# Second MLP product by seven block products in place of eight, with the residual kept in DRAM

## Chip, core and metric

The kernel runs on one core of one Trainium2 chip. The metric is device microseconds of one execution; the value is the median of three runs. All times below are microseconds (us) unless marked ns. PE is the matrix engine (TensorE), PEld its weight loads, DVE is VectorE, ACT is ScalarE, POOL is GpSimd, and SP (SyncE) issues nearly all DMA transfers.

## What is computed

One decoder layer in float32: 512 tokens, 1024 channels. Three token mixers and an output projection come first; the change lies behind them, in the residual and the MLP of 4096 hidden columns.

```python
    x = x + rms_norm(merged @ w_out[l], g_mix_post[l])
    h = rms_norm(x, g_ff_pre[l])
    ff = jnp.square(jax.nn.relu(h @ w_ff_in[l])) @ w_ff_out[l]
    x = x + rms_norm(ff, g_ff_post[l])
```

## The kernel before

**Products.** Each operand is split into two float32r parts, hi (a cast on ACT) and lo (the rest, by a subtraction on DVE). `mm3` makes a product of three matmuls: hi·hi, hi·lo, lo·hi, each with 128 rows of contraction, 128 output rows and 512 output columns.

**Weights.** `plan` lists all weights in the order of use, in chunks of 512 KB. `load_chunk` loads a chunk into one of three buffers `raw` (RAW = 3); `split_chunk` makes `whi` (ACT) and `wlo` (DVE) in one of six buffer pairs (HL = 6) and then asks for the next load, which takes the `raw` buffer just read. `Weights` splits three chunks ahead of the one in use (AHEAD = 3).

**MLP.** The hidden columns are taken in four blocks b of 1024. The first product of a block (PSUM tile `psf`, eight tiles f of 128 hidden columns by 512 tokens, 24 matmuls each) goes through `ff_act`: relu on ACT, square on DVE, split into `ah` and `al`. The second product (PSUM tile `acc`) runs over two column halves and four token tiles of 128, 192 matmuls a block; `ff_done` adds each result into `ys` in SBUF. After the last block, each token tile is scaled by its root mean square and added to `x1`, the residual, which stays in SBUF from the output projection to the end. In block 0 the first four tiles f run by token halves, since the second 256 tokens are still being normed.

**Order.** PE takes its instructions in program order throughout; ACT and DVE do so from the second half of the output projection until tile f = 3 of block 0 (`act.on = dve.on = False` ends it). From there a scheduler sets their order, which is then fixed: each engine runs its queue in that order. Buffers are rings: slots `main`, `out` and `tmp` (12 slots for temporaries) in SBUF, eight banks in PSUM. Everything that goes through the recording helper has line 77.

Of the kernel before, what the change touches and what calls it, by code (L numbers as in the profile page):

```python
# [48 lines left out]
def trunk_layer(ctx: ExitStack, tc: tile.TileContext, x, w_in, w_pool, pool_scale, gm_gain,  # L49
# [8 lines left out]
    sb = ctx.enter_context(tc.tile_pool(name="sb", bufs=1))  # L58
    sm = ctx.enter_context(tc.tile_pool(name="sm", bufs=4))

    # One slot is [128, 512] of four bytes; a tag is a ring of slots that later phases take over.
    RINGS = {"main": 18, "out": 16, "tmp": 12, "nb": 2, "be": 2}

    def slot(ring, name, dt=F32):
        return sb.tile([P, T], dt, name=name, tag=ring, bufs=RINGS[ring])

    class InOrder:
        """An engine that, while `on`, takes its instructions in the order of this program."""
# [31 lines left out]

    def plan_cols(w, c0, n=256):
# [43 lines left out]
    for b in range(NB):  # L145
        for f in range(0, FT, 2):
            use["f1", b, f] = plan_cols(ff_in_k, (b * FT + f) * P)
        for hf in range(2):
            use["f2", b, hf] = plan_cols(ff_out_k[:, b * FT:(b + 1) * FT, :], hf * 512, 512)
# [12 lines left out]
    def split_chunk(engines="v"):  # L162
        raw = loaded[len(made)]
        hi = wp.tile([P, CHUNK], F32R, name="whi", bufs=HL)
        lo = wp.tile([P, CHUNK], F32R, name="wlo", bufs=HL)
        for n, e in enumerate(engines):
            c = slice(n * CHUNK // len(engines), (n + 1) * CHUNK // len(engines))
            act.copy(hi[:, c], raw[:, c])
            (nc.gpsimd if e == "p" else dve).tensor_sub(lo[:, c], raw[:, c], hi[:, c].bitcast(F32))  # L169
        at = 0  # L170
        outs = []
        for v in plan[len(made)]:
            _, a, b = v.shape
            outs.append(tuple(t[:, at:at + a * b].rearrange("p (a b) -> p a b", a=a)
                              for t in (hi, lo)))
            at += a * b
        made.append(outs)
        if len(loaded) < len(plan):
            load_chunk()

    class Weights:
        """The k tiles of one use; its chunks, and AHEAD more, are split as they come up."""
# [9 lines left out]
        def __getitem__(self, k):  # L192
            i, j = self.tiles[k]
            live = self.chunks.start if self.keep else i
            while len(made) < min(len(plan), i + 1 + self.ahead, live + HL):
                split_chunk()
            h, l = made[i][self.part]
            return h[:, j, :], l[:, j, :]

# [1 line left out]
    def split(src, hi, lo, scale=None):  # L201
        """hi, lo <- src (times a per-partition scale) in two float32r parts."""
# [8 lines left out]
    def mm3(ps, left, right, first, last):  # L211
        (lh, ll), (rh, rl) = left, right
        pe.matmul(ps, lhsT=lh, rhs=rh, start=first, stop=False)
        pe.matmul(ps, lhsT=lh, rhs=rl, start=False, stop=False)
        pe.matmul(ps, lhsT=ll, rhs=rh, start=False, stop=last)
# [4 lines left out]
    def rstd(parts, n, name):  # L220
        """1 / rms over n of rows whose sums of squares come in parts."""
# [16 lines left out]
    def rms(xt):  # L238
        """1 / rms of the rows of [128 tokens, D], in two halves."""
# [16 lines left out]
    def split_to(hT, pt, t, g):  # L256
        """Half g of the columns t of the transposed, split activations."""
# [16 lines left out]
    psum = ctx.enter_context(tc.tile_pool(name="psum", bufs=1, space=PSUM))  # L274
# [6 lines left out]
    # the gain's row above rows of zeros: a product with ones spreads it over the partitions  # L281
# [29 lines left out]
    def act_pair():  # L311
        return tuple(sb.tile([P, KD, T], F32R, name=f"hT{n}", tag=f"hT{n}", bufs=1)
                     for n in range(2))

    if True:
# [10 lines left out]
        def v_part(t, c, which):  # L326
            """Token tile t against chunk c of v's weights: the products with hi, the others."""
# [58 lines left out]
        def qk_pair(hp):  # L386
            """q as [hi; lo] and [lo; hi], k as [hi; hi] by head, and k's lo parts."""
# [19 lines left out]
        def stick_scores(hp, i):  # L407
            """nb = 1 - beta, be = beta, then be <- beta times the later keys' 1 - beta."""
# [11 lines left out]
            for j in range(2):  # L420
# [3 lines left out]
                # both neutral where the key isn't before the query  # L424
# [9 lines left out]
        def stick_transpose(i, be):  # L434
            """[keys, key tile, hi | lo, queries]"""
# [22 lines left out]
        def attention(fill):  # L458
            """Every pair and query tile in turn, with fill(n) between the stages."""
# [193 lines left out]
        def branch(w, e, rhs, sg):  # L653
            """sg *= one branch's product."""
# [11 lines left out]
        def merge_two(dd):  # L666
            """The gated pooling and spatial gating branches of two channel tiles."""
# [25 lines left out]
        def alongside(work, other, every):  # L693
            """work, with a step of other after every few of its own."""
# [32 lines left out]
    gfpost = bcast_row(g_ff_post[0], [wide("gfpost", F32)[:, :T] for _ in range(2)])  # L727
# [3 lines left out]
    def bank4(which, i, name):  # L731
        """Bank i of one of two sets of four."""
# [41 lines left out]
    def residual(t, r):  # L774
        """x1 += yg / rms, and its squares' sums."""
# [3 lines left out]
        for g in range(2):  # L779
            square_sum(x1[t][g], ssq[:, g:g + 1])  # L780
        return ssq
# [16 lines left out]
    def between(t, k):  # L798
        """Transpositions, weights and norms that go along with token tile t."""
# [21 lines left out]
    def ff_act(ps):  # L821
# [9 lines left out]
    yg = [[None, None] for _ in range(NT)]  # L831

    def finish_out(t):
        r = rstd_d(twos[t], "p")
        rows = slice(t * P, (t + 1) * P)
        for g, c in (0, WHOLE), *((1, c) for c in (HALVES if t == NT - 1 else (WHOLE,))):
            dve.scalar_tensor_tensor(x1[t][g][:, c], yg[t][g][:, c], r, x1[t][g][:, c], ALU.mult,
                                     ALU.add)
            nc.sync.dma_start(o2[rows, g * T + c.start:g * T + c.stop], x1[t][g][:, c])

    for b in range(NB):
        aT = []
        first = 0
        if b == 0:
            # the first tiles take the tokens that are ready before the others
# [4 lines left out]
            for f in range(first):  # L850
                ff_in(pss[f], wks[f // 2], f % 2, halves[0])
                if f in (1, 2):
                    turn(f + 1)
            for f in range(first):
# [3 lines left out]
                aT.append(ff_act(pss[f]))  # L858
            act.on = dve.on = False
        for f in range(first, FT):  # L860
            if f % 2 == 0:
                wk = Weights(("f1", b, f))
            ps = bank4("mm", f, "psf")
            ff_in(ps, wk, f % 2, slice(0, T))
            aT.append(ff_act(ps))

        def ff_done(hf, b=b):
            def done(t, ps, c):
                if b == 0:
                    ys[t][hf] = slot("out", "ys")  # L870
                    act.copy(ys[t][hf], ps)
                    return
                y = ys[t][hf]
                dve.tensor_add(y[:, c], ps[:, c], y[:, c])
                if b < NB - 1:
                    return
                n = hf + (c.start > 0)
                square_sum(y[:, c], twos[t][:, n:n + 1])
                if c.start == 0:
                    yg[t][hf] = slot("tmp", "yg")  # L880
                dve.tensor_mul(yg[t][hf][:, c], y[:, c], gfpost[hf][:, c])
                if hf and c.stop == 512:
                    finish_out(t)
            return done

        for hf in range(2):
            final = b == NB - 1 and hf == 1
            token_gemm(aT, ("f2", b, hf), ("acc", "mm")[hf], ff_done(hf), final,
                       last=HALVES if final else (WHOLE,))
# [29 lines left out]
```

## Time and profile before

| | |
|---|---|
| median of three runs (lowest, highest) | 734.59 us (733.43, 735.8) |
| the profiled execution (its span) | 733.6 us |
| PE busy | 719.6 us, 98% |
| DVE busy | 393.6 us, 54% |
| ACT busy | 298.5 us, 41% |
| granted PE clock, mean | 0.996 of full speed |
| HBM read, written | 70.33 MB, 2.10 MB |

The span runs from the first to the last instruction of the profiled execution; the page gives no other time for it. Matmuls overlap in the pipeline, so the busy share of PE says that PE always had a matmul in it, and the time of a stretch divided by its matmuls is what one of them costs.

### The profile page before, as it was taken

Reading aid. Unit: us, or ns where it says so; the run is one execution under the profiler, and the core shown is the slowest. Engines: PE = TensorE matmul, PEld = TensorE weight load, DVE = VectorE, ACT = ScalarE, POOL = GpSimd, SP = SyncE. Lnnn points to the kernel's source line nnn. Section 1 sums busy time; section 2 is a strip of 40 time slices with the busy share of each in tenths; the row PEclk is TensorE's granted clock in tenths of the full one; section 3 lists DMA queues with packets and bytes.
Section 4 is the critical chain, followed back from the end, with each engine's and each line's share of the span. In section 5 each row is a group of like instructions: output and inputs, shape, how many; then the busy total and the mean of one; then the engine's idle time right before and its main releaser. Section 6 shows DMA issues by size and latency. Waiting matters only on the chain.

```text
span 733.6 us, 8878 instructions
## 1 busy us (share of the span) xinstructions
PE 719.6 (98%) x3428; PEld 596.8 (81%) x3428; DVE 393.6 (54%) x587; ACT 298.5 (41%) x505; POOL 53.9 (7%) x103
## 2 busy tenths in 40 slices
PE   7999999999999999999999999999999999999996
PEld 4889887787878888888889888888888888888885
DVE  5745799777868444351685632244334443444345
ACT  5566656655444233221444532434212432133311
POOL 3100222211121000000130000000000000000000
PEclk9999999999999999999999999999999999999999
DMA  8273311322225323451212433233333233224002
GB/s 280 67 205 86 113 59 59 107 66 70 75 76 154 115 86 87 115 201 58 86 58 92 138 115 89 86 114 104 97 87 114 77 98 113 87 86 116 29 24 91
DMA packets 63404, 73.00 MB, mean 100 GB/s; under 512 B 3201, under 2 KB 48385, under 8 KB 63362
## 3 DMA queue, kind: packets, MB, share of 16 engines
q1 hardware_dynamic: 63360, 72.43, 32.6%
q8 instruction: 27, 0.44, 0.2%
q14 instruction: 15, 0.12, 0.1%
q10 hardware_dynamic: 2, 0.00, 0.0%
HBM read 70.33 MB, written 2.10 MB: 99 GB/s over the span
## 4 chain that ended last, share of the span: by engine, by line
PE 94%; DVE 2%; ACT 1%; issue 1%; DMA 1%; POOL 1%; SPq 0%; POOLq 0%; DVEq 0%; ACTq 0%
PE acc L77 29%; PE psc L77 26%; PE psf L77 23%; PE psb L77 6%; PE psv L77 3%; PE psgv L77 2%; PE z L77 1%; PE pt L77 1%; PE av L77 1%; PE trx L77 1%; DMA raw<-in_w_in_dram 1%; ACT junk L77 0%; POOL wlo L169 0%; PE pmix L77 0%; DVE nb L77 0%
## 5 line engine op out<-in xcount | busy, mean ns | idle before, releaser
L77 DVE TENSOR_TENSOR wlo<-raw,whi 128x1024 fp32r<-128x1024 f32 (+1 forms) x121 | 146.2, 1212 | 184.5 <-ACT whi L77 184.3
L77 ACT CAST whi<-raw 128x1024 fp32r<-128x1024 f32 (+1 forms) x128 | 128.5, 1013 | 177.1 <-PE acc L77 93.7
L77 PE MATMUL psc<-hT,whi 128*128 128x512 f32 x576 | 182.1, 397 | 0.0
L77 PE MATMUL psf<-hT,whi 128*128 128x512 f32 (+1 forms) x576 | 161.2, 366 | 0.0
L77 PEld LDWEIGHTS psc<-hT,whi 128*128 128x128 f32 x576 | 103.8, 188 | 21.0 <-issue 1.5
L77 PEld LDWEIGHTS psf<-hT,whi 128*128 128x128 f32 x576 | 104.1, 189 | 17.5
L77 PE MATMUL psc<-hT,wlo 128*128 128x512 f32 x288 | 112.5, 391 | 0.0
L77 PE MATMUL psf<-hT,wlo 128*128 128x512 f32 (+1 forms) x288 | 105.2, 365 | 0.0
L77 PE MATMUL acc<-wlo,ah 128*128 128x512 f32 (+1 forms) x264 | 101.0, 383 | 0.0
L77 PE MATMUL acc<-whi,al 128*128 128x512 f32 (+1 forms) x264 | 101.0, 383 | 0.0
L77 PE MATMUL acc<-whi,ah 128*128 128x512 f32 (+1 forms) x264 | 101.0, 383 | 0.0
L77 PEld LDWEIGHTS psc<-hT,wlo 128*128 128x128 f32 x288 | 54.1, 188 | 11.8
L77 PEld LDWEIGHTS psf<-hT,wlo 128*128 128x128 f32 x288 | 54.3, 189 | 8.7
L77 PEld LDWEIGHTS acc<-wlo,ah 128*128 128x128 f32 x264 | 49.6, 188 | 9.8
L77 PEld LDWEIGHTS acc<-whi,ah 128*128 128x128 f32 x264 | 49.6, 188 | 9.7
L77 PEld LDWEIGHTS acc<-whi,al 128*128 128x128 f32 x264 | 49.6, 188 | 9.6
L77 DVE TENSOR_TENSOR rl<-rl 128x512 f32<-128x512 f32 x32 | 21.9, 688 | 35.2 <-ACT rl L77 35.2
L229 POOL TENSOR_TENSOR pr<-pv,mhalf 128x1 f32<-128x1 f32 x8 | 4.8, 606 | 482.0 <-DVE pv L77 482.0
L77 ACT ACTIVATE rl<-psf 128x512 f32<-128x512 f32 x32 | 18.9, 593 | 38.4 <-PE psf L77 38.4
L77 DVE TENSOR_TENSOR al<-rl,ah 128x512 fp32r<-128x512 f32 x32 | 22.1, 692 | 19.9 <-ACT ah L77 19.9
L77 ACT CAST ah<-rl 128x512 fp32r<-128x512 f32 x32 | 19.8, 620 | 31.7 <-DVE rl L77 31.7
L77 DVE TENSOR_TENSOR_SCAN nb<-nb,zeros 128x128 f32<-128x128 f32 (+3 forms) x32 | 27.5, 863 | 7.5 <-POOL nb L426 7.1
(158 smaller groups left out, 811.0 us busy)
## 6 DMA issues: line engine op xcount, KB each, us to landing
raw<-in_w_in_dram SPq DMA_DIRECT2D x42, 512.0 KB, 3.9
raw<-in_w_ff_in_dram SPq DMA_DIRECT2D x32, 512.0 KB, 3.8
raw<-in_w_ff_out_dram SPq DMA_DIRECT2D x32, 512.0 KB, 3.9
xt<-in_x_dram SPq DMA_DIRECT2D x16, 256.0 KB, 6.3
raw<-in_w_out_dram SPq DMA_DIRECT2D x8, 512.0 KB, 3.8
raw<-in_w_br_sb_dram SPq DMA_DIRECT2D x4, 512.0 KB, 3.7
out_dram<-xt SPq DMA_DIRECT2D x7, 256.0 KB, 2.1
raw<-in_w_br_pool_dram SPq DMA_DIRECT2D x4, 256.0 KB, 3.0
```

Of the source, the lines that this page charges most:

```text
L77: i = op(*args, **kw).ins
L229: nc.gpsimd.tensor_tensor(r, v, mhalf, ALU.pow)
```

## The change

Per block the second product is written as a two by two block product: hidden tiles in pairs m (even tile, odd tile), tokens in halves (0 to 255, 256 to 511), output columns in halves of 512. Seven products of block sums take the place of eight, in four stages: s1 (PSUM `x`, `z`), s2 (`y`), s3 (into `x` again, and a new `y`), s4 (into `z` and `x` again). A stage has 48 matmuls, s2 24. The names below are `accx`, `accy`, `accz`; there are two of each, p = 0 and 1, for two token tiles.

- Weight sums are made on DVE from each loaded chunk (`block_sums`), and pieces of `w_ff_out` are loaded again for later stages: 14 chunks of 512 KB a block in place of 8.
- `ff_act` now works by pair: relu and square on ACT into `ec`, then four sums of 256 columns on DVE (`q`, `n`, `s`, `r`), splits of 768 columns (three blocks) and 1024 columns (the sums).
- `gather` adds PSUM into `ys`: 16 additions a block in place of 8. In block 0 the first for each piece is a copy on ACT.
- PSUM gets a new pool `psum2` (tags f, x, y, z of two banks each) after tile f = 3 of block 0; SBUF gets a new pool `ff` over the memory of the old one, in which `tmp` has 4 slots in place of 12. A tile of a new pool waits for the old tiles that lay there.
- The residual `x1` is written to DRAM in `residual` (eight transfers of 256 KB) and read back in the last block as `x1b` (four transfers of 512 KB, into the two `ec` buffers).
- `RINGS["tmp"] = 4` holds `rl`, and at the end `junk` (the target of the sums of squares) and `yg` (a tile's scaled output, which is also what is written out).

```diff
+        for stage in ("s1", "s2", "s3", "s4"):
+            use[stage, b] = range(len(plan), len(plan) + (2 if stage == "s2" else FT // 2))
...
+                if stage == "s2":
+                    plan.append([ff_out_k[:, b * FT + 2 * m + 1:b * FT + 2 * m + 4:2, :512]])
+                else:
+                    plan.append({"s1": [b11, b12], "s3": [b22, b21], "s4": [b12, b22]}[stage])
+                    derive[len(plan) - 1] = (stage, m)
...
+        if stage == "s1":
+            t1s[m] = ff.tile([P, T], F32, name="t1", bufs=4)
+            dve.tensor_add(t1s[m], one, two)
+            return [one, t1s[m]]
+        if stage == "s3":
+            dve.tensor_add(one, one, t1s[m])
+            dve.tensor_add(two, two, one)
+        else:
+            dve.tensor_add(one, one, two)
+        return [raw]
...
+            sp.dma_start(x1d[t][:, g * T:(g + 1) * T], x1[t][g])
...
         rl = slot("tmp", "rl")
         act.activation(rl, ps, AF.Relu)
-        dve.tensor_mul(rl, rl, rl)
-        a = slot("main", "ah", F32R), slot("main", "al", F32R)
-        split(rl, *a)
-        return a
+        act.activation(ec[:, 2 * odd:2 * odd + 2, :].rearrange("p a t -> p (a t)"), rl, AF.Square)
+        if not odd:
+            return
+        a21, a11, a22, a12, q, n, s, r = (ec[:, i, :] for i in range(8))
+        hi, lo = (ff.tile([P, 7, 256], F32R, name=x, bufs=FT // 2) for x in ("ah", "al"))
+        split(ec[:, 1:4, :], hi[:, :3, :], lo[:, :3, :])
+        dve.tensor_sub(q, a21, a22)
+        dve.tensor_sub(n, q, a11)
+        dve.tensor_sub(s, a11, a21)
+        dve.tensor_add(r, n, a12)
+        split(ec[:, 4:, :], hi[:, 3:, :], lo[:, 3:, :])
...
+        if ys[t][hf] is None:
+            ys[t][hf] = ff.tile([P, T], F32, name="ys", tag="ys", bufs=8)
+            act.activation(ys[t][hf], ps, AF.Copy, scale=1.0 if op == ALU.add else -1.0)
+        else:
+            dve.tensor_tensor(ys[t][hf][:, c], ys[t][hf][:, c], ps[:, c], op)
...
+            early.close()
+            ff = ctx.enter_context(tc.tile_pool(name="ff", bufs=1, reuse_waits="tile"))
+            home[0] = ff
+            RINGS["tmp"] = 4
...
+            banks.close()
+            psum = ctx.enter_context(tc.tile_pool(name="psum2", bufs=1, space=PSUM,
+                                                  reuse_waits="tile"))
...
+        for m in range(M):
+            for j, ps, part in (0, x, A11), (1, z, AQ):
+                for p in two:
+                    product(ps[p], part, p, m, w(m, j))
+        for p in two:
+            gather(2 + p, 0, x[p], ALU.add, b)
+            gather(p, 1, z[p], ALU.add, b)
+        y = [block("y", p) for p in two]
...
+        for m in range(M):
+            product(z[0], AR, 0, m, w(m, 1), False)
+        gather(2, 1, z[0], ALU.add, b)
+        scaled_out(2, 1)
+        for p in two:
+            for m in range(M):
+                product(x[p], AS, p, m, w(m, 0), False)
+            gather(p, 1, x[p], ALU.subtract, b)
+            gather(p, 0, x[p], ALU.add, b)
+            scaled_out(p, 1)
+            scaled_out(p, 0)
+            if p == 0:
+                finish_out(2)
+            finish_out(p)
+        for c in HALVES:
+            for m in range(M):
+                product(z[1], AR, 1, m, w(m, 1), False, c)
+            gather(3, 1, z[1], ALU.add, b, c)
+            scaled_out(3, 1, c)
+        finish_out(3)
```

**Where instructions stand.** PE's queue is the same up to tile f = 4 of block 0. There, before and after, ACT's queue from the relu of f = 0 on reads as follows (`psf_3577` to `psf_3580`, after `psf_3590` to `psf_3593`, are the tiles f = 0 to 3; `whi` casts are weight chunks; `raw_3758` is the last chunk of the first product after the change, `raw_3764` and `raw_3771` the first two of s1).

```order
L77 ACTIVATE rl_3729<-psf_3577 128x512 [waits PE_49,Activation_49]
L77 CAST ah_3732<-rl_3729 128x512 [waits DVE_49]
L77 CAST whi_3736<-raw_3336 128x1024 [waits DMAHW4_49]
L77 CAST whi_3742<-raw_3508 128x1024 [waits DMAHW5_49]
L77 CAST whi_3748<-raw_3558 128x1024 [waits DMAHW6_49,PE_49]
L77 CAST whi_3754<-raw_3740 128x1024 [waits DMAHW7_49,PE_49]
```

```order
L82 CAST whi_3774<-raw_3758 128x1024 [waits DMAHW7_49,PE_49]
L82 ACTIVATE rl_3805<-psf_3591 128x512 [waits DMAHW5_49,PE_49]
L82 CAST whi_3900<-raw_3764 128x512 [waits DMAHW0_49,PE_49,Pool_49]
L82 ACTIVATE ec_3750<-rl_3805 128x512 [waits Activation_49]
L82 CAST whi_3966<-raw_3771 128x512 [waits DMAHW2_49,PE_49,Pool_49]
L82 CAST ah_3808<-ec_3750 128x768 [waits DMAHW6_49,DMAHW3_49,Activation_49]
L82 CAST whi_3900<-t1_3902 128x512 [waits DVE_49]
L82 CAST whi_3966<-t1_3968 128x512 [waits DVE_49]
L82 CAST ah_3808<-ec_3750 128x1024 [waits DVE_49]
L82 ACTIVATE rl_3843<-psf_3592 128x512
L82 ACTIVATE ec_3842<-rl_3843 128x512 [waits Activation_49]
L82 ACTIVATE rl_3870<-psf_3593 128x512 [waits PE_49]
```

The first matmul of tile f = 4 (`accf_3887`, in the first bank of `psum2`) waits on ACT, to the count that `rl_3870` brings, the relu of f = 3; that relu stands behind the cast of all four sums of pair 0 (`ah_3808`, 1024 columns), which waits for the sum `r` on DVE. Before, tile f = 4 took the bank of f = 0.

DVE's queue after, in s1 of block 1, up to the lo part of the sums of pair 3 (`al_4683`; `ec_4650` are its sums, `raw_4704`, `raw_4723`, `raw_4742`, `raw_4763` the chunks of s3, in which sums with s1's `t1` are made):

```order
L82 TENSOR_TENSOR wlo_4758<-raw_4704,whi_4757 128x1024 [waits Activation_49]
L82 TENSOR_TENSOR raw_4742<-raw_4742,t1_4630 128x512 [waits DMAHW0_49]
L82 TENSOR_TENSOR ec_4650<-ec_4650 128x256 [waits DVE_49]
L82 TENSOR_TENSOR wlo_4785<-raw_4723,whi_4784 128x1024 [waits Activation_49]
L82 TENSOR_TENSOR raw_4742<-raw_4742 128x512 [waits DMAHW1_49,DVE_49]
L82 TENSOR_TENSOR raw_4763<-raw_4763,t1_4698 128x512 [waits DMAHW2_49]
L82 TENSOR_TENSOR al_4683<-ec_4650,ah_4682 128x1024 [waits Activation_49]
```

`al_4683`, which the last pair of s1 needs, stands behind sums of s3's weights that wait for their loads; before, DVE had only `wlo` and additions into `ys` there. Further on, the gathers of s2's `accy` stand behind a sum for s4's second chunk (`raw_4811`) in the same way.

ACT's queue at the end: `junk` takes a `tmp` slot, and where the slot was a `yg`, it waits for that tile's write to DRAM (DMAHW).

```order
L82 ACTIVATE junk_6265,two1_3169<-ys_4144 128x512 [waits DVE_49,Activation_49]
L82 ACTIVATE junk_6269,two1_3169<-ys_4279 128x512 [waits DMAHW6_49,DMAHW5_49,DVE_49]
L82 ACTIVATE junk_6296,two3_3171<-ys_4277 128x256 [waits DMAHW7_49,DMAHW4_49,DVE_49]
L82 ACTIVATE junk_6313,two3_3171<-ys_4277 128x256 [waits DMAHW0_49,DVE_49,Activation_49]
L1078 UNCONDITIONAL_BRANCH
```

```order
L77 ACTIVATE junk_5897,two1_3164<-ys_4245 128x512 [waits DVE_49,Activation_49]
L77 ACTIVATE junk_5937,two2_3165<-ys_4253 128x512 [waits DVE_49,Activation_49]
L77 ACTIVATE junk_5977,two3_3166<-ys_4261 128x256 [waits DVE_49,Activation_49]
L77 ACTIVATE junk_6007,two3_3166<-ys_4261 128x256 [waits DVE_49,Activation_49]
L915 UNCONDITIONAL_BRANCH
```

The first of these is after, the second before, where no sum of squares waits for a transfer. In the program the three waits are for the writes of token tile 0's two halves and of token tile 1's first half.

## Rows read from the trace of the kernel before

**Rows 1.** Page, busy time, share of the span and instructions.

```profile
PE 719.6 (98%) x3428; PEld 596.8 (81%) x3428; DVE 393.6 (54%) x587; ACT 298.5 (41%) x505; POOL 53.9 (7%) x103
```

**Rows 2.** Chain that ended last, in order: start us, us, what.

```profile
421.62 43.52 PE acc L77 x192
465.14 43.52 PE psf L77 x192
...
682.74 43.84 PE acc L77 x216
726.60 0.44 DVE ys L77
...
730.01 0.40 DVE xt L77
```

**Rows 3.** Groups by shape: busy us, mean ns, idle before and its releaser.

```profile
L77 DVE TENSOR_TENSOR wlo<-raw,whi 128x1024 fp32r<-128x1024 f32 x116 | 141.5, 1224 | 183.9 <-ACT whi L77 183.7
L77 ACT CAST whi<-raw 128x1024 fp32r<-128x1024 f32 x116 | 121.7, 1053 | 175.6 <-PE acc L77 93.7 <-PE psc L77 30.9 <-PE psf L77 29.0
L77 DVE TENSOR_TENSOR ys<-acc,ys 128x512 f32<-128x512 f32 x23 | 15.5, 689 | 16.5 <-PE acc L77 16.5
L77 DVE TENSOR_TENSOR sg<-sg 128x512 f32<-128x512 f32 x16 | 11.0, 687 | 0.3
L77 ACT ACTIVATE junk<-xt 128x512 f32<-128x512 f32 x16 | 10.1, 630 | 12.9 <-DVE xt L77 12.1 <-DMA xt<-in_x_dram 0.7
L77 DVE TENSOR_TENSOR a<-pt,a 128x256 fp32r<-128x256 f32 x8 | 3.4, 425 | 4.9 <-ACT a L77 4.8
```

**Rows 4.** DVE in order of time, block 1's first product: start us, us, instruction.

```profile
476.96 1.23 DVE L77 TENSOR_TENSOR wlo<-raw,whi 128x1024 fp32r<-128x1024 f32 x1 [1.50 <-ACT whi L77]
478.10 0.69 DVE L77 TENSOR_TENSOR rl<-rl 128x512 f32<-128x512 f32 x1
```

**Rows 5.** ACT and DVE in order of time, block 0.

```profile
391.29 0.60 ACT L77 ACTIVATE rl<-psf 128x512 f32<-128x512 f32 x1 [5.23 <-PE psf L77]
...
393.17 2.95 ACT L77 CAST whi<-raw 128x1024 fp32r<-128x1024 f32 x3
394.25 3.49 DVE L77 TENSOR_TENSOR wlo<-raw,whi 128x1024 fp32r<-128x1024 f32 x3 [0.26 <-ACT whi L77]
399.40 1.05 ACT L77 CAST whi<-raw 128x1024 fp32r<-128x1024 f32 x1 [3.28 <-DMA raw<-in_w_ff_in_dram]
...
401.20 1.05 ACT L77 CAST whi<-raw 128x1024 fp32r<-128x1024 f32 x1 [0.25 <-DMA raw<-in_w_ff_out_dram]
```

**Rows 6.** DMA issues: queue, form, count, KB each, median us to landing.

```profile
raw<-in_w_ff_out_dram SPq DMA_DIRECT2D x32, 512.0 KB, 3.9
out_dram<-xt SPq DMA_DIRECT2D x7, 256.0 KB, 2.1
raw<-in_w_br_pool_dram SPq DMA_DIRECT2D x4, 256.0 KB, 3.0
raw<-in_w_br_gm_dram SPq DMA_DIRECT2D x4, 256.0 KB, 3.3
```

**Rows 7.** Stretches: us, busy by engine, PEclk, DMA share, GB/s.

```profile
7.40:10.10 2.70, 0.66 (x4) 0.42 (x4) 1.57 (x4) 2.70 (x8) 1.46 (x2) 1.00 1.04 394
...
11.50:12.50 1.00, 1.00 (x4) 0.81 (x3) 1.00 (x1) 1.00 (x3) 1.00 (x1) 0.50 1.06 395
...
13.50:14.50 1.00, 1.00 (x4) 0.71 (x4) 1.00 (x3) 0.00 (x0) 0.85 (x1) 0.50 0.51 185
...
380.00:384.00 4.00, 3.35 (x28) 3.15 (x27) 2.70 (x7) 2.35 (x6) 0.55 (x1) 1.00 0.45 131
```

**Rows 8.** End of the last block in order of time: root mean square and scaling.

```profile
711.52 0.16 DVE L77 SCALAR_TENSOR_TENSOR pv<-two,pv 128x1 f32<-128x1 f32 x1
...
711.82 0.55 POOL L229 TENSOR_TENSOR pr<-pv,mhalf 128x1 f32<-128x1 f32 x1 [328.61 <-DVE pv L77]
712.40 1.41 DVE L77 SCALAR_TENSOR_TENSOR xt<-yg,pr,xt 128x512 f32<-128x512 f32 x2 [0.66 <-POOL pr L229]
```

More of the change, by code (lines that the diff above doesn't have):

```diff
@@ L165, in split_chunk @@
         lo = wp.tile([P, CHUNK], F32R, name="wlo", bufs=HL)
[L166 to L169, printed above, removed]
+        if len(made) in derive:
+            pieces = block_sums(raw, *derive[len(made)])
+        else:
+            pieces = [raw[:, n * CHUNK // len(engines):(n + 1) * CHUNK // len(engines)]
+                      for n in range(len(engines))]
+        at = 0
+        for n, piece in enumerate(pieces):
+            c = slice(at, at + piece.shape[1])
+            at = c.stop
+            e = engines[n % len(engines)]
+            act.copy(hi[:, c], piece)
+            (nc.gpsimd if e == "p" else dve).tensor_sub(lo[:, c], piece, hi[:, c].bitcast(F32))
         at = 0
@@ L179, in split_chunk, with block_sums @@
             load_chunk()
+    t1s = {}
+    def block_sums(raw, stage, m):
+        one, two = raw[:, :512], raw[:, 512:]
+        if stage == "s1":
[8 more added lines that the diff above has]
+        return [raw]
     class Weights:
@@ L196, in __getitem__ @@
                 split_chunk()
+        def __getitem__(self, k):
+            i, j = self.tiles[k]
+            self.ready(i)
             h, l = made[i][self.part]
@@ L209, in split, with mm3 @@
                                            ALU.subtract)
-    def mm3(ps, left, right, first, last):
+    def mm3(ps, left, right, first, last, more=False):
         (lh, ll), (rh, rl) = left, right
-        pe.matmul(ps, lhsT=lh, rhs=rh, start=first, stop=False)
-        pe.matmul(ps, lhsT=lh, rhs=rl, start=False, stop=False)
-        pe.matmul(ps, lhsT=ll, rhs=rh, start=False, stop=last)
+        pe.matmul(ps, lhsT=lh, rhs=rh, start=first, stop=False, skip_group_check=more)
+        pe.matmul(ps, lhsT=lh, rhs=rl, start=False, stop=False, skip_group_check=more)
+        pe.matmul(ps, lhsT=ll, rhs=rh, start=False, stop=last, skip_group_check=more)
     def cut(pair, s):
@@ L726, in trunk_layer @@
     gfpre = bcast_row(g_ff_pre[0], [slot("be", "gfpre") for _ in range(2)])
-    gfpost = bcast_row(g_ff_post[0], [wide("gfpost", F32)[:, :T] for _ in range(2)])
+    x1d = [dram.tile([P, D], F32, name=f"x1d{t}") for t in range(NT)]
     SETS = {"mm": ("mm", "mm", "mm", "av"), "acc": ("z", "z", "tr", "tr")}
@@ L831, in trunk_layer, with product, block, gather @@
     yg = [[None, None] for _ in range(NT)]
+    x1b = [None] * NT
+    def product(ps, part, p, m, weights, new=True, c=WHOLE):
+        left = tuple(x[:, part, p * P:(p + 1) * P] for x in parts[m])
+        mm3(ps[:, c], left, cut(weights, c), new and m == 0, new and m == M - 1, not new)
+    def block(which, p):
+        return psum.tile([P, T], F32, name="acc" + which, tag=which, bufs=2)
+    def gather(t, hf, ps, op, b, c=WHOLE):
+        if ys[t][hf] is None:
+            ys[t][hf] = ff.tile([P, T], F32, name="ys", tag="ys", bufs=8)
+            act.activation(ys[t][hf], ps, AF.Copy, scale=1.0 if op == ALU.add else -1.0)
+        else:
+            dve.tensor_tensor(ys[t][hf][:, c], ys[t][hf][:, c], ps[:, c], op)
+    def scaled_out(t, hf, c=WHOLE):
+        n = hf + (c.start > 0)
+        square_sum(ys[t][hf][:, c], twos[t][:, n:n + 1])
+        if c.start == 0:
+            yg[t][hf] = slot("tmp", "yg")
+        dve.tensor_mul(yg[t][hf][:, c], ys[t][hf][:, c], gfpost[hf][:, c])
     def finish_out(t):
@@ L853, in trunk_layer @@
                     turn(f + 1)
+            early.close()
+            ff = ctx.enter_context(tc.tile_pool(name="ff", bufs=1, reuse_waits="tile"))
+            home[0] = ff
+            RINGS["tmp"] = 4
+            gfpost = bcast_row(g_ff_post[0], [ff.tile([P, T], F32, name=f"gfpost{g}")
+                                              for g in range(2)])
             for f in range(first):
@@ L862, in trunk_layer @@
                 wk = Weights(("f1", b, f))
-            ps = bank4("mm", f, "psf")
+            ps = block("f", f)
             ff_in(ps, wk, f % 2, slice(0, T))
[L865 to L889, printed above, removed]
+            ff_act(f, ps)
+        final = b == NB - 1
+        if final:
+            for i in range(2):
+                pair = ff.tile([P, 2, D], F32, name="x1b", tag="ec", bufs=2)
+                for t in (2 * i, 2 * i + 1):
+                    x1b[t] = pair[:, t - 2 * i, :]
+                    sp.dma_start(x1b[t], x1d[t])
@@ new lines, in stage, with tile_of @@
+        def stage(name, n, keep=False):
+            wk = Weights((name, b), keep=keep)
+            wk.tiles = [(i, j, k) for i in use[name, b] for j in range(len(plan[i]))
+                        for k in range(plan[i][j].shape[1])]
+            return lambda m, j: tile_of(wk, m * n + j)
+        def tile_of(wk, i):
+            i, j, k = wk.tiles[i]
+            wk.ready(i)
+            h, l = made[i][j]
+            return h[:, k, :], l[:, k, :]
+        two = range(2)
+        x, z = ([block(w, p) for p in two] for w in "xz")
@@ new lines, in trunk_layer @@
+        w = stage("s1", 2)
+        for m in range(M):
[6 more added lines that the diff above has]
+        y = [block("y", p) for p in two]
+        w = stage("s2", 1)
+        for m in range(M):
+            for p in two:
+                product(y[p], A12, p, m, w(m, 0))
+        for p in two:
+            gather(2 + p, 0, y[p], ALU.add, b)
@@ new lines, in trunk_layer @@
+        if final:
+            for p in two:
+                scaled_out(2 + p, 0)
+        y = [block("y", p) for p in two]
+        w = stage("s3", 2)
+        for m in range(M):
+            for j, ps, part in (0, x, AN), (1, y, A22):
+                for p in two:
+                    product(ps[p], part, p, m, w(m, j), j == 1)
+        for p in two:
+            gather(2 + p, 1, x[p], ALU.subtract, b)
+            gather(p, 0, y[p], ALU.add, b)
+        w = stage("s4", 2, final)
+        if not final:
+            for m in range(M):
+                for j, ps, part in (1, z, AR), (0, x, AS):
+                    for p in two:
+                        product(ps[p], part, p, m, w(m, j), False)
+            for p in two:
+                gather(2 + p, 1, z[p], ALU.add, b)
+                gather(p, 1, x[p], ALU.subtract, b)
+                gather(p, 0, x[p], ALU.add, b)
+            continue
@@ new lines, in trunk_layer @@
+        for m in range(M):
+            product(z[0], AR, 0, m, w(m, 1), False)
+        gather(2, 1, z[0], ALU.add, b)
+        scaled_out(2, 1)
+        for p in two:
+            for m in range(M):
+                product(x[p], AS, p, m, w(m, 0), False)
+            gather(p, 1, x[p], ALU.subtract, b)
+            gather(p, 0, x[p], ALU.add, b)
+            scaled_out(p, 1)
[4 more added lines that the diff above has]
+        for c in HALVES:
+            for m in range(M):
+                product(z[1], AR, 1, m, w(m, 1), False, c)
+            gather(3, 1, z[1], ALU.add, b, c)
+            scaled_out(3, 1, c)
```

42 lines of the change are left out of this document (29 added, 13 removed).

## Prediction

> **What bounds the kernel now.** I read the busy line of the page first: PE is busy for 98% of the span, DVE for 54%, ACT for 41% [rows 1]. Then the chain that ended last, to see what a piece of PE's work costs: in the MLP each product of a block is one step of 192 matmuls in 43.52 us, so 43.52 / 192 = 0.2267 us a matmul, with no gap between steps, and behind the last step come 733.6 - 726.58 = 7.0 us of tail [rows 2]. The groups by shape give the length of each operation on DVE and ACT; the idle time ahead of `wlo` there, 184 us, nearly all released by ACT's casts, says that DVE mostly waits for its next chunk [rows 3]. So the kernel is bound by PE's count of matmuls, and whatever makes PE wait is added in full. DVE's rows in order show that an operation costs the queue less than its row: a `wlo` of 1.23 us is followed by the next start 1.14 us later, 0.09 less than its length [rows 4]. By the same difference 512 columns cost about 0.60 us, 256 about 0.33 (from the 0.42 of the 256-column row in [rows 3]), and 768, for which there is no row, between 0.60 and 1.14, so 0.87.
>
> **Removed: 96 matmuls.** Per block 168 in place of 192, so 4 x 24 x 0.2267 = -21.8 us. The other matmuls keep their shape and price.
>
> **Added: a wait ahead of tile f = 4 in block 0.** The order rows show PE's first matmul of f = 4 waiting for the relu of f = 3, and that relu behind the cast of pair 0's four sums in ACT's queue. Before, f = 4 started when f = 3 was done: 421.62 is the end of the product before, and four tiles of 24 matmuls lie between, so 421.62 - 4 x 5.44 = 399.86. After, the relu of f = 0 is at 391.29 as before and three weight casts and lo parts follow as in [rows 5]; with a square in between the lo parts end at about 394.8, 395.9 and 397.0. The first frees the `raw` buffer for the last chunk of the first product. A chunk of 512 KB takes 3.9 us from issue to landing [rows 6], so it is there at 398.7, cast at 399.8, its lo part done at 401.0 (before, the same chain shows a cast at 399.40, 3.9 us after 394.25 + 1.23). Then come on DVE, ahead of the sum `r` and its split, in the queue of after: eight operations of 512 columns (8 x 0.60), four of 256 (4 x 0.33) and one of 768 (0.87), together 7.0: 408.0. ACT casts the 1024 columns (1.05, 409.1), then relu, square, relu (0.60 each, 410.8 with their hand-overs). PE waits from 399.86 to 410.8: +10.9 us. If chunks land in 3.0 us, as pieces of 256 KB do [rows 6], it is 9.9; if they take what the second cast in [rows 5] shows (its buffer freed one `wlo` later, at 396.6, its cast at 401.20, so 4.6 us), and the s1 chunks too, 13. I take the middle, as 3.9 is the median of 32.
>
> **Added: a slow start after that wait.** After the first phase's idle stretch (7.4 to 10.1 us, PE busy for 0.66 of 2.7 us, with the clock still granted in full) the granted clock was 0.50, the 1.2 GHz level, from about 11.5 to 14.5 us, and four matmuls took 1 us there; around 380 us, where PE pauses for under a microsecond at a time, it stayed 1.00 [rows 7]. A pause of 10.9 us is more like the first. Some 3.3 us at half the rate lose 1.7 us (0 if nothing drops, 3.4 at twice the time). The Trainium skill, "TensorE: Matmul & The Clock Gate", section "HAM oscillation — how this bites in real kernels", says the same of idle gaps between bursts of matmuls, that the array falls back to half its clock; the trace agrees [rows 7], and without such a fall the sum would be 1.7 us less.
>
> **Added: stalls in the four second products.** By its instructions and these pitches DVE has work for about 29 of 38 us there, so it isn't short of time; its queue order is what counts. Time is from the start of s1. The buffer pair for s2's second chunk comes free at 0, its cast ends at 1.05, and DVE goes on at 1.08 with its `wlo` (1.14), two sums for s3 (0.60 each), a sum and a split of pair 3 (0.33, 0.87), another sum (0.33) and the split of s3's first chunk (1.23), in all 5.1; with 0.45 of waits for ACT's casts between them it is at 6.63. That releases the load of s3's fourth chunk, whose first 256 KB are there after 3.05: 9.68. Its sum (0.60) and the 1024-column lo part of pair 3 behind it (1.23) end at 11.5. PE needs that part at 3 x 2.72 + 1.36 (pair 3's first two products) + 0.45 = 9.97. Stall: 1.6 us. Further on the first addition of s2's `accy` stands behind the sum for s4's second chunk: its buffer is free at 14.47 (s3's third split), + 3.9 = 18.4, + 0.60 + 0.69 = 19.7; s3 asks for the bank at 19.3 (10.88 + 1.6 + 5.44 + 1.36): 0.4. Block 0 has copies on ACT for the first additions, so 1.6; blocks 1 and 2 have 2.0 each; in block 3 the second 1 MB of the residual queues ahead of s3's chunk, for which I add about 1 us: 3.0. Sum +8.6. With the loads hidden it is 0.6 a block (2.5), with loads of 4.6 us about 4.2 a block (17).
>
> The Trainium skill, "DMA: Bandwidth & Descriptors", section "Anatomy of one DMA — SWDGE (gpsimd) path", fits a transfer as about 2.0 us plus bytes over 436 GB/s; as an estimate that is 2.6 us for 256 KB and 3.2 for 512 KB, less than the 3.0 to 3.3 and 3.9 of [rows 6], and it would bring this term down to about 5. For this queue the rows decide.
>
> **Changed: the tail.** Before, 7.0 us lie behind the last matmul. After, ACT's sums of squares write into slots that hold a tile's output until it has gone out, so three writes (2.1 us each [rows 6]) come in a chain. From the start of s4 in block 3: nominally the last matmul ends at 11.0, but its last pieces wait for DVE's additions until 12.6; token tile 0's scaling ends at 13.3; its write lands at 15.4; two squares of tile 1 (0.63 each [rows 3]), `pv` and the power on POOL (712.40 - 711.52 = 0.9 [rows 8]) and two scalings (1.41) bring 19.3; the write of that lands at 21.4; square of 256 columns and the same power, 23.1; three scalings, 24.5; from there 3.2 to the end of the span, as now (733.6 - 730.41). That is 27.7 - 11.0 = 16.7 in place of 7.0: +9.7 us. With only one write on the path it is about 3.5; with slower hand-overs 11.
>
> **Costed at nothing.** 24 more chunk loads (12.6 MB) and 4 MB of residual out and back: about 190 GB/s in a second product, while 394 GB/s were moved between 7.4 and 10.1 us [rows 7]; if loads get slower by it, that is the 4.6 us of the bounds. The residual's writes stand on SP's queue ahead of one chunk, whose cast comes later anyway. Squares on ACT in place of DVE lie under PE's work, and ACT is idle more than half of the time.
>
> **Sum.** 733.6 - 21.8 + 10.9 + 1.7 + 8.6 + 9.7 = 742.7, and the median of the runs is 1.0 above this execution: 743.7 us.
>
> **Rivals.** B, loads land as late as the overlapped one did (4.6 us): +2 at f = 4 and up to +8.4 in the stages, about 752. The 24 more loads speak for it, the median of 3.9 against. C, faster: tile f = 4 waits for no more than the relu (0.7 us), because DVE and ACT get through pair 0 before PE is done with f = 3; then no slow start either, 743.7 - 10.2 - 1.7 = 731.8. It decides once the wait with its slow start is under about 10 us in all, where the total falls to that of before less 0.3%. Against it: `r` can't be summed before the chunk loaded at 394.8 has been split. D, balance: stalls at 2.5 and a tail with about 6 us more, 743.7 - 6.1 - 3.7 = 733.9. The count of matmuls alone, with every wait hidden, would be 712.8; the order rows speak against that.
>
> **How the numbers follow.** The forecast with its own range of 738 to 749 has 0.58, B 0.18, C 0.09, D 0.08; 0.03 are left for faster still, 0.04 for slower than B. A difference under 0.3% can't be told from none here, so 732.4 to 736.8 is the same: faster 0.12, same 0.08, slower 0.80. From 733 to 755 leaves out C, the two rests and a little of B, just under 0.2.
>
> **What would show it.** Right: PE idle for about 11 us ahead of tile f = 4 of block 0, released by ACT, a granted clock of 0.5 behind it; PE idle for 1 to 3 us in the last pair of each s1, released by DVE's `al`; 0.2267 us a matmul elsewhere; some 15 to 17 us from the last matmul to the end, with sums of squares released by writes to the output. Wrong: f = 4 starts on time, s1 runs through, or one write alone is waited for in the tail; or chunks land well before 3 or after 4.6 us.

## The result and the profile after

The changed kernel takes 756.52 us (median of four runs, 756.2 to 757.06), before 735.0: ratio 1.029 (95% interval 1.028 to 1.031). It is slower, as forecast, but by 21.5 us in place of 9.1, and 1.5 us above the top of the range of 733 to 755. Its profiled execution has a span of 754.8 us, 21.2 more than [rows 1]'s.

First the busy line of the page after, which answers to [rows 1]. PE has 108 matmuls fewer (the 96, and 12 because fewer are cut in two column pieces at the end) and is busy for only 3.5 us less; DVE is busy for 101 us more.

```profile
PE 716.1 (95%) x3320; PEld 579.5 (77%) x3320; DVE 494.7 (66%) x755; ACT 353.5 (47%) x577; POOL 53.8 (7%) x103
```

PE's waits, over the whole execution (line, what it waited for, us in total, times, longest). The first is the wait before tile f = 4; `accz <- al` is the wait in the last pair of s1, once a block; `accz <- ys` is the wait of the last pieces of s4 for DVE's additions, 1.7 us before the last matmul ends. The rows left out are waits of `warm`, `psv`, `trx` and `pt` of up to 1.8 us, which the kernel before has as well.

```profile
PE accf L82 <- ACT rl L82: 11.9, 1, 11.9
PE accz L82 <- DVE al L82: 5.0, 4, 1.9
...
PE accz L82 <- DVE ys L82: 1.3, 1, 1.3
...
PE accy L82 <- DVE ys L82: 0.2, 1, 0.2
```

ACT in order of time (start, us, instruction, idle before it and who ended it): the second cast is that of pair 0's four sums. The relu in the last row, that of f = 3, ends at 415.18 and releases PE, whose next matmul starts at 415.23, as the order rows ahead of the prediction said.

```profile
402.32 1.05 ACT L82 CAST whi<-raw 128x1024 fp32r<-128x1024 f32 x1 [3.33 <-DMA raw<-in_w_ff_in_dram]
...
412.49 1.04 ACT L82 CAST ah<-ec 128x1024 fp32r<-128x1024 f32 x1 [4.23 <-DVE ec L82]
413.44 0.59 ACT L82 ACTIVATE rl<-psf 128x512 f32<-128x512 f32 x1
414.06 0.63 ACT L82 ACTIVATE ec<-rl 128x512 f32<-128x512 f32 x1
414.60 0.58 ACT L82 ACTIVATE rl<-psf 128x512 f32<-128x512 f32 x1
```

Windows there (from:to, length, PE busy and matmuls, granted clock, DMA share, GB/s). The clock is at 0.50 until 420.4, so 12 matmuls take 5.2 us; then 17 take 3.4.

```profile
410.00:415.00 5.00, 0.00 (x0) 0.50 0.25 90
415.20:420.40 5.20, 5.17 (x12) 0.50 0.01 3
420.60:424.00 3.40, 3.40 (x17) 1.00 0.00 0
```

The chain that ended last. It has three writes of the output. Behind the second and the third stands a sum of squares that waited for the landing, as predicted; the first lies ahead of the last matmul, which ends at 739.84, and holds up a scaling on DVE, for 0.3 us. The first row here is the surprise. It is a projection long before the MLP, in code that the change left alone, and its 48 matmuls take 11.16 us.

```profile
235.42 11.16 PE psc L82 x48
...
733.08 2.06 DMA out_dram<-yg
...
735.23 0.60 DVE yg L82
...
740.29 2.05 DMA out_dram<-yg
...
742.44 0.73 ACT junk L82 x2
...
746.19 2.05 DMA out_dram<-yg
...
748.34 0.42 ACT junk L82
```

The same projection in the kernel before takes 10.88 us, 0.2267 a matmul:

```profile
235.04 10.88 PE psc L77 x48
```

In the MLP it is the same: a first product's step of 179 matmuls takes 41.60 us, 0.2324 each, where [rows 2] had 0.2267, at a granted clock of 1.00 in both.

```profile
481.01 41.60 PE accf L82 x179
```

In steady steps a matmul with 512 columns costs about 0.0058 us more, from the first products on.

### The profile page after: what moved, and what is told of

It reads as the page before. It is cut to its first block, busy times and chain, and to the rows that moved or that the text cites. A ratio compares the mean times of both kernels' runs of the same rounds, so it can differ in the third digit from the quotient of the medians.

```text
span 754.8 us, 9132 instructions
## 1 busy us (share of the span) xinstructions
PE 716.1 (95%) x3320; PEld 579.5 (77%) x3320; DVE 494.7 (66%) x755; ACT 353.5 (47%) x577; POOL 53.8 (7%) x103
## 4 chain that ended last, share of the span: by engine, by line
PE 81%; DVE 8%; DMA 7%; ACT 2%; issue 1%; POOL 0%; SPq 0%; DVEq 0%; POOLq 0%; ACTq 0%
PE psc L82 26%; PE accf L82 19%; PE psb L82 6%; PE acc L82 5%; PE accy L82 5%; PE accx L82 5%; DMA raw<-in_w_ff_out_dram 4%; PE accz L82 3%; PE psv L82 3%; DVE wlo L82 2%; PE psgv L82 2%; PE z L82 1%; PE pt L82 1%; DVE raw L82 1%; PE av L82 1%
## 5 line engine op out<-in xcount | busy, mean ns | idle before, releaser
L82 PE MATMUL accf<-hT,whi 128*128 128x512 f32 x448 | 142.4, 399 | 11.9 <-ACT rl L82 11.9
L82 PEld LDWEIGHTS accf<-hT,whi 128*128 128x128 f32 x448 | 85.3, 191 | 32.5 <-ACT rl L82 12.1
L82 PE MATMUL accf<-hT,wlo 128*128 128x512 f32 x224 | 89.3, 399 | 0.0
L82 PEld LDWEIGHTS accf<-hT,wlo 128*128 128x128 f32 x224 | 42.7, 191 | 10.3
L82 ACT CAST ah<-ec 128x768 fp32r<-128x768 f32 (+1 forms) x32 | 30.2, 943 | 32.6 <-DVE ec L82 32.1
L82 DVE TENSOR_TENSOR al<-ec,ah 128x768 fp32r<-128x768 f32 (+1 forms) x32 | 34.8, 1088 | 9.6 <-ACT ah L82 9.6
L82 PE MATMUL accx<-whi,al 128*128 128x512 f32 x96 | 37.9, 395 | 0.0
L82 PE MATMUL accx<-wlo,ah 128*128 128x512 f32 x96 | 37.9, 395 | 0.0
L82 PE MATMUL accx<-whi,ah 128*128 128x512 f32 x96 | 37.9, 395 | 0.0
L82 DVE TENSOR_TENSOR ec<-ec 128x256 f32<-128x256 f32 x64 | 26.7, 422 | 14.4 <-ACT ec L82 14.1
```

The costliest lines, as they stand in the source:

```text
L82: i = op(*args, **kw).ins
```

## The experiments

Two theories on that price. **P**: it is set by where the operands lie in SBUF. The change moved pools: `hT` has its own (`ht`), the small tiles (`sm`, 1408 bytes a partition) now come ahead of it and of all rings behind it, while the weight buffers (`wp`) stay where they were. **R**: it comes with the rest of the changed program or with the execution.

**e1: only the places.**

```diff
-    sb = ctx.enter_context(tc.tile_pool(name="sb", bufs=1))
     sm = ctx.enter_context(tc.tile_pool(name="sm", bufs=4))
+    ht = ctx.enter_context(tc.tile_pool(name="ht", bufs=1))
+    sb = ctx.enter_context(tc.tile_pool(name="sb", bufs=1))
...
-        return tuple(sb.tile([P, KD, T], F32R, name=f"hT{n}", tag=f"hT{n}", bufs=1)
+        return tuple(ht.tile([P, KD, T], F32R, name=f"hT{n}", tag=f"hT{n}", bufs=1)
```

> The kernel before, its work unchanged, with the pools in the order of the changed kernel: the small tiles, then the activations hT, then the rest, so that every tile of the first phases lies where the changed kernel has it. In the changed kernel a 512-column matmul costs 0.2325 us from the first phase on, before 0.2267. If the place of the operands in SBUF sets that price (theory P), it is 0.2325 here too and the time about 735 + 2,900 x 0.0058 = 752 us. If it comes with the rest of the changed program or with the execution (theory R), it stays 0.2267 and the time 735.

Measured: 746.28 us, before 733.81 (733.41 to 735.72). The chain of e1, which answers to [rows 2], in all its 512-column steps:

```profile
234.76 11.15 PE psc L78 x48
...
425.09 44.61 PE acc L78 x192
469.70 44.62 PE psf L78 x192
```

44.61 / 192 = 0.2323. Theory P holds: with no instruction changed, only the place, the kernel before loses 12.5 us. The time expected for P was 752, 5.7 us too much, since not all of the 2,900 matmuls lose the full 0.0058 us: in the short pieces of the projections one already cost 0.229 us before (15 in 3.43 us, 3.48 here).

**e2: the residual written to DRAM as well, in the kernel before.** A DRAM tile `x1d` and the `sp.dma_start` of the change's `residual`, nothing more.

> The kernel before, which in addition writes the residual to DRAM in eight transfers of 256 KB (nothing reads them). By theory P the price of a matmul stays 0.2267 us and the time is 735. If the DRAM tile in the program raises the price of every matmul (one form of theory R), 0.2325 and 752 us. If the writes on SP's queue delay the chunk behind them, PE waits up to 1 us before tile f = 4 and the time is up to 736.

Measured: 733.61 us. In this one run the writes and the DRAM tile cost nothing that can be told from the spread of the kernel before, as the prediction costed them.

**e3: other PSUM banks for f = 4 and 5**, in the changed kernel.

```diff
+            y0 = [block("y", p) for p in range(2)]
         for f in range(first, FT):
...
-        y = [block("y", p) for p in two]
+        y = [block("y", p) for p in two] if b else y0
```

> The changed kernel with the new PSUM banks dealt so that tiles f = 4 and 5 of block 0 lie where transpositions were, not where f = 3 was. If the bank alone makes the wait of 11.9 us (theory bank), PE runs through and the time falls by 11.9 and the 2.9 us of half clock to about 742. If the queue behind pair 0 is what is late (theory queue), the wait moves to tile f = 6, which needs the relu of f = 4: that relu would come at about 420, f = 4 and 5 end at 414, so some 6 us are left, and the time is about 748 to 751, depending on whether the clock drops.

Measured: 748.09 us (ratio to before 1.019, 1.015 to 1.023). PE in order of time has the wait at tile f = 6, with half of its length, released by a relu in the queue behind pair 0, so theory queue:

```profile
420.93 1.22 PE L82 MATMUL accf<-hT,whi 128*128 128x512 f32 x2 [6.25 <-ACT rl L82]
```

**e4: no wait for a write at the end**, in the changed kernel.

```diff
-        square_sum(ys[t][hf][:, c], twos[t][:, n:n + 1])
+        junk = wp.tile([P, CHUNK], F32, name="raw", bufs=RAW)
+        act.activation(junk[:, :c.stop - c.start], ys[t][hf][:, c], AF.Square,
+                       accum_out=twos[t][:, n:n + 1])
         if c.start == 0:
-            yg[t][hf] = slot("tmp", "yg")
+            yg[t][hf] = (slot("tmp", "yg") if t >= 2 else
+                         ff.tile([P, T], F32, name="yg", tag="t1", bufs=4))
```

> The changed kernel with the sums of squares of the end going into the raw buffers and the scaled outputs into eight slots of their own, so that nothing waits for a write of the output. My step on the tail: the 15.1 us behind the last matmul fall to about 7.5, as before, and the time to about 749. Rival: the work itself (additions, squares, powers) takes that long and the writes lie beside it; then the tail stays over 12 us and the time at 754 or more.

Measured: 745.36 us (1.015, 1.011 to 1.019). No transfer ends an ACT wait in the tail any more, and from the last matmul (734.2) to the end of the span (743.7) 9.5 us pass in place of 15.0. So my step on the tail holds for most of it, and the rival (over 12 us) falls. That is 5.5 of the 11.2 us won. Another 4 come from shorter waits in the second products (2.5 us in place of 6.5): 3.4 of them in s1, which the edit doesn't touch by itself, and why they shrank isn't shown; some 2 us are not assigned.

**e5: the changed kernel with 128 unused bytes ahead of `hT`.** In the compiled programs the places are:

```
                          weight buffers from   hT from   offset modulo 256
before                          33824            128032          0
after, e1, e3, e4               33824             84384        128
e5                              33824             84512          0
e6 (before, all + 128)          33952            128160          0
e7 (e1 + 384)                   33824             84768          0 (256 modulo 512)
e9 (e1 + 192)                   33824             84576         64
```

```diff
+    gap = ctx.enter_context(tc.tile_pool(name="gap", bufs=1))
+    nc.gpsimd.memset(gap.tile([P, 32], F32, name="gap"), 0.0)
     ht = ctx.enter_context(tc.tile_pool(name="ht", bufs=1))
```

> The changed kernel with 128 unused bytes ahead of hT, so that all tiles behind the weight buffers lie at the same offset from them, modulo 512 bytes, as in the kernel before. If the offset between the two operands, or the address itself, modulo 256 or 512 bytes sets the price of a matmul (theory P), a 512-column matmul is back at 0.2267 us and the time falls by 2,900 x 0.0057, some 11 us of it on PE's own path in the MLP and 3 to 5 ahead of it, to about 741 to 745. If the price depends on a larger modulus or on which pool comes first, it stays 0.2325 and 756.

Measured: 742.39 us (1.011, 1.009 to 1.013). The whole change otherwise, and 14.1 us less. The projection is back at its price, and the waits are those of the changed kernel, some of them shorter; first its chain, then PE's waits in the MLP:

```profile
233.83 10.88 PE psc L84 x48
```

```profile
PE accf L84 <- ACT rl L84: 11.6, 1, 11.6
PE accz L84 <- DVE al L84: 3.1, 4, 1.3
PE accz L84 <- DVE ys L84: 1.5, 1, 1.5
PE accy L84 <- DVE ys L84: 0.6, 3, 0.2
```

**e6, e7 and e9: which offset**, in the kernel before. e6 puts 128 unused bytes ahead of the weight buffers, so all operands move together; e7 and e9 are e1 with 384 and 192 unused bytes ahead of `hT`.

> The kernel before with 128 unused bytes ahead of the weight buffers, so that all operands move by 128 bytes together. If the offset between an operand and the other counts, a matmul stays at 0.2267 us and the time at 734. If the address of each counts (32 modulo 256 is good, 160 is not), it is 0.2325 or more and the time 746 or more.

> The kernel before with the pools in the order of the changed one, and 384 unused bytes ahead of hT: the offset between hT and the weight buffers is then a multiple of 256 bytes and not of 512. With 256 bytes as the period a 512-column matmul costs 0.2267 us and the time is 734; with 512 it stays 0.2325 and the time is 746.

> The kernel before with the pools in the order of the changed one and 192 unused bytes ahead of hT: the offset between hT and the weight buffers is 64 modulo 256 bytes, where 0 gave 0.2267 us a matmul and 128 gave 0.2325. If any offset other than 0 costs the same, 0.2325 us and 746; if the price grows with the offset, about 0.229 and 740; if only 128 clashes, 0.2267 and 734.

Measured: e6 733.3, e7 735.38, e9 745.91 us. The same step of the second product in the chains of e7 and of e9:

```profile
422.04 43.52 PE acc L80 x192
```

```profile
236.10 10.99 PE psc L80 x48
...
424.67 44.79 PE acc L80 x192
```

So it isn't the address itself (e6), and an offset of 256 modulo 512 is as good as 0 (e7). At an offset of 64 a matmul takes 0.2333 us in most of the MLP's steps, but 0.2290 in some projections (10.99 / 48) and in one step of the MLP (43.96 / 192). The time of e9 is that of its first case (746), but not with one price; both offsets other than 0 that were tried cost 0.002 to 0.007 us a matmul more, and what decides within that range is open.

The same traces hold products of 256 columns with one operand in the weight buffers and one in `hT`. They do not get dearer, but a little cheaper; the same 84 matmuls, first before, then e1 (offset 128), then e9 (64):

```profile
60.60 10.08 PE psgv L77 x84
```

```profile
59.32 9.96 PE psgv L78 x84
```

```profile
61.88 9.55 PE psgv L80 x84
```

**e8: the causes together.** The 128 bytes of e5, the end of e4, and banks for f = 4 to 7 that nothing late holds:

```diff
-            ps = block("f", f)
+            ps = y0[7 - f] if b == 0 and f >= 6 else block("f", f)
```

> The changed kernel with the 128 unused bytes, the end of e4 and PSUM banks for tiles f = 4 to 7 of block 0 that nothing late holds (the two of accy serve f = 6 and 7). If the terms add up (my theory of four causes: the price of a matmul, the wait before f = 4 with its slow start, the tail, the stalls in s1), 756.5 - 13 - 15 - 7.5 = 721, with some 5 us of stalls in s1 to s3 left; faster than before by about 2%. Rival: taking one wait away moves it to the next place (s1, whose pairs 0 and 1 now come from a queue that is late by 10 us); then PE waits in s1 of block 0 and the time is 730 or more.

Measured: 733.54 us, ratio 0.9998 (0.9982 to 1.0014): the same as before, so the rival. PE's waits and the windows of e8 (in these, PE, PEld, DVE, ACT and POOL busy, then the clock) show that they moved from f = 4 to s1 of block 0, and the slow start with them: nine matmuls in the last 7 us, with two waits among them.

```profile
PE accz L84 <- DVE al L84: 4.6, 4, 1.6
PE accx L84 <- DVE al L84: 2.9, 1, 2.9
...
PE accz L84 <- ACT ah L84: 1.4, 1, 1.4
```

```profile
400.00:428.00 28.00, 27.53 (x122) 22.46 (x121) 21.15 (x35) 17.41 (x27) 0.00 (x0) 1.00 0.33 108
428.00:436.00 8.00, 4.99 (x16) 2.95 (x14) 6.34 (x10) 4.17 (x6) 0.00 (x0) 0.81 0.40 132
436.00:443.00 7.00, 4.32 (x9) 2.98 (x10) 6.14 (x8) 4.67 (x7) 0.00 (x0) 0.50 0.48 166
```

Of the 21.8 us that the 96 matmuls were worth, PE's waits in the MLP take back 11.0, the tail 2.2 (9.2 us in place of 7.0) and the half clock, at 13 matmuls, some 2.6; the profiled execution is 2.7 us under [rows 1]'s, so about 3 us are not assigned.

**e11: VectorE in program order through the MLP**, in e8: the line `act.on = dve.on = False` becomes `act.on = False`.

> The kernel of e8, with VectorE kept to the order of the program through the MLP too, so that no sum for s3's weights stands ahead of a lo part that s1 needs. If the queue order made by the scheduler holds s1 up (my term 4, here 12 us of waits and of half clock in block 0 and 5 us in the others), PE runs through s1, and the time falls from 733.5 to 718 to 724, 2% under the kernel before. Rival: VectorE has too much to do between the relu of f = 0 and s1 of block 0, whatever the order; then a wait of 5 us or more stays in block 0 and the time is 728 or more.

Measured: 792.77 us (1.078, 1.074 to 1.083), far worse. DVE now stands behind casts that ACT, still scheduled, makes later, and PE behind DVE. DVE's waits, then PE's:

```profile
DVE al L84 <- ACT ah L84: 82.9, 32, 8.5
DVE wlo L84 <- ACT whi L84: 52.7, 39, 6.5
```

```profile
PE accy L84 <- DVE ys L84: 27.0, 4, 7.6
PE accx L84 <- DVE wlo L84: 13.9, 5, 5.5
```

The forecast falls: the scheduler's queue is better than this one. The rival's time holds, but not its reason, since DVE waits for casts here. Whether a third order would free s1 wasn't tried.

**e12 and e13: sums of weight blocks on GpSimd**, in e8: `nc.gpsimd.tensor_add` in place of `dve.tensor_add` in `block_sums`, all of them or those of s3 and s4.

> The kernel of e8 with all sums of weight blocks on GpSimd in place of VectorE (512 columns cost it about 1.35 us, by its rows before, in place of 0.69). If s1 is held up because VectorE's queue has lo parts behind sums that wait for loads (my term 4 as a mechanism), the waits in s1 go in all blocks: 733.5 less some 10 us in block 0 and 3 us in the others, 718 to 723. Rival: the slower sums, each twice as long and two in a row in s3, make the weights themselves late; then PE waits for whi or wlo and the time is 733 or more.

> As e12, but only the sums of s3 and s4 on GpSimd; those of s1, on which pair 0 waits in block 0, stay on VectorE. If VectorE's queue order is the cause, 716 to 722, with s1's weights no later than in e8. If the rival holds, 733 or more, with waits for weights in s3.

Measured: 744.42 (1.013, 1.011 to 1.015) and 740.67 us (1.009, 1.006 to 1.012). Neither forecast came true. The rival's time (733 or more) did, but not by the waits that it named; others came. DVE itself became slower, as the groups by shape show, first of e8, then of e12:

```profile
L84 DVE TENSOR_TENSOR ec<-ec 128x256 f32<-128x256 f32 x64 | 26.7, 421 | 10.1 <-ACT ec L84 9.8
```

```profile
L84 DVE TENSOR_TENSOR ec<-ec 128x256 f32<-128x256 f32 x64 | 41.9, 659 | 11.9 <-ACT ec L84 11.0
...
L220 POOL TENSOR_TENSOR raw<-raw 128x512 f32<-128x512 f32 x16 | 28.6, 1791 | 1.3
```

The Trainium skill, "GPSIMD Engine Reference", section "1. Specifications", says that GpSimd shares its way to SBUF with VectorE and that the two contend when VectorE's instruction has two operands in SBUF; the trace agrees, 659 ns in place of 421. In block 1 of e12 a 768-column lo part takes 0.96 us at 505.12, with GpSimd idle, and 2.04 at 516.82, where it ends 0.8 us after the GpSimd sum that was running when it began (516.69 to 518.04). In e12 PE waits 12.2 us for DVE's additions into `ys` that free `accy`, ahead of s3, in e13 9.7. The wait in the last pair of s1 stays, with no sum in DVE's queue: 0.8, 0.8 and 1.0 us in blocks 1 to 3, where e8 has 0.6, 1.6 and 1.1. As DVE was slower at the same time, these runs don't decide whether the order of its queue holds s1 up.

## Why the prediction was wrong

- **The step that failed** is "The other matmuls keep their shape and price" under the 96 removed. The shape stayed; the price of a 512-column matmul in steady steps went from 0.2267 to 0.2325 us (0.2333 in later blocks of some runs), from the first products to the end. In the kernel before, with only the places changed, this costs 12.5 us (e1). Taking only the places back brings the changed kernel down by 756.52 - 742.39 = 14.1 us (e5), some 12.9 of them the price, as the sum below shows. That e5 then stands 1.3 us from the forecast of 743.7 is in part luck: the waits and the slow start were undersized, the stalls oversized. I read the diff of the pools for who waits for whom, not for where the tiles lie. No rival held it either.
- **The wait ahead of f = 4**, +10.9: 11.9 measured, 11.6 in e5, by the mechanism forecast; about 0.6 of the difference is DVE's wait for s1's first load (idle until 405.21), which the sum of operations left out. e3 adds that the bank is only the place where it shows: the chain of loads, splits and sums is late by some 10 us, and a free bank moves the wait on, to f = 6 in e3 and to s1 in e8.
- **The slow start**, +1.7: a granted clock of 0.50 for 5.2 us of matmuls costs half of that, 2.6. It was undersized, since I took its length (3.3 us) from the first phase.
- **The stalls**, +8.6: 5.2 us of waits (5.0 in s1 and 0.2 for `accy`), 3.7 in e5, so oversized; the bank of `accy` costs next to nothing, and the last block 1.9 in s1 in place of 3.0. The mechanism is in the chain of block 1, where s1 starts at 525.46:

```profile
532.10 2.97 DMA raw<-in_w_ff_out_dram
...
535.09 0.69 DVE raw L82
535.78 1.15 DVE al L82
...
536.98 1.21 PE accz L82 x4
```

The prediction put the landing 9.68 and the end of the lo part 11.5 us behind the start of s1, which is 535.1 and 537.0; they are at 535.07 and 536.93. PE waits 1.1 us there, 1.6 were forecast. The loads kept to the short times, as the page's row on them shows, and rival B, which needs 4.6, fell by that; that its 752 is the nearest to the time is luck.

```profile
raw<-in_w_ff_out_dram SPq DMA_DIRECT2D x96, 256.0 KB, 3.0
```

- **The tail**, +9.7: from the last matmul at 739.8 to 754.8 are 15.0 us, so +8.0, and with the 1.3 us that the last pieces wait for DVE, which the prediction counted here, +9.3 (9.2 in e5). Two of the three writes, of 2.05 us each, lie behind the last matmul. e4 shows that without these waits 2.5 us stay over the 7.0 of before.
- **Costed at nothing**: the residual's writes are free as far as one run shows (e2). The more loads and the squares on ACT were not tried apart.
- **The sum of e5**, on its span: -21.8 + 11.6 + 2.6 + 3.7 + 9.2 (its tail of 14.7 and 1.5 of waits ahead of it) = 5.3, against 740.0 - 733.6 = 6.4; 1.1 us are not assigned. In the changed kernel the same terms are -21.8 + 11.9 + 2.6 + 5.2 + 9.3 = 7.2; its span is 14.8 above e5's, 1.9 of it by those terms, which leaves 12.9 for the price: 20.1 of the 21.2. e1, from the start of the first step of 96 matmuls to its last matmul, is also 12.9 us longer than the kernel before.
- **C and D**: f = 4 waited in full, and neither the stalls nor the tail fell to their low ends.

## What to carry to other kernels

A price per instruction that is taken from a trace holds for operands where they lay; where an edit adds or reorders pools, compare the offsets of the operands that meet in one instruction, before and after, and a cheap test is the kernel before with only the pools moved. Where a wait ends a chain that is late as a whole, freeing the buffer moves the wait to the next place (f = 4, f = 6, s1), and here a saving of 22 us on the bound engine was gone with some 10 us of lateness at each of two ends, even at the old price (e5). In a ring, look for a slot that is written out by a transfer: who takes it next waits for the landing, 2 us here.

## What was not expected of the hardware

In steady steps a 512-column float32r matmul took 0.2267 us when its two operands lay at a multiple of 256 bytes from each other within a partition, and 0.2290 to 0.2333 us at offsets of 64 and 128, at a granted clock of 1.00 throughout; moving both by 128 changed nothing. Each of the products that fill the MLP and the projections has one operand in the weight buffers and one behind the moved pools, so both kinds (weights held or streamed) showed it. Products of 256 columns didn't lose by it: 0.1200 us a matmul at 0, 0.1186 at 128, 0.1137 at 64. What in the chip does it, which further offsets cost how much, and whether other types show it, no run here tells. The other thing is VectorE's 256-column additions at 659 ns in place of 421 beside a busy GpSimd.
